# Modulation transposes issued as a later step, and the last head's gate products moved ahead of the third scan's drain

## The chip, the cores and the metric

The kernel runs on one core of one Trainium2 chip. Time is device time in microseconds (us) from start to end of one execution; several executions are timed and the median is given. The engines are TensorE (PE, with its weight loads as PEld), VectorE (DVE), ScalarE (ACT), GpSimd (POOL) and SyncE (SP), which issues nearly all loads.

## The reference, cut to what matters

Two layers run over 128 context tokens and 512 latent tokens, with a model width of 1024. Each layer is a SwiGLU block, a mixer and a second SwiGLU block, each behind a norm with a scale, a shift and a gate that come from a conditioning vector (two of them: one for context, one for latent tokens).

```python
def adaln_params(cond, w, b):                 # w is 1024 x 9216 in each layer
    m = jax.nn.silu(cond) @ w + b
    return m.reshape(cond.shape[0], N_MOD, 1, D_MODEL)      # nine slots: shift, scale, gate, three times

def swiglu(h, w_in, w_out):
    gt, up = jnp.split(h @ w_in, 2, axis=-1)
    return (jax.nn.silu(gt) * up) @ w_out

# even layer: mixer = [conv module || two-way HGRN2 scan of four heads], one projection in, one out
    o = o_f + rev(o_b)
    o = rms_norm(o, norm_g) * jax.nn.silu(g.reshape(B, T, HG_HEADS, HG_VDIM))
    out = jnp.concatenate([a, r], axis=-1) @ w_out
```

The odd layer's mixer is windowed attention; the change doesn't touch it.

## The kernel before

All activations stay on the chip, transposed: feature on the partition, 640 tokens along the row. Products are made in a split form: each fp32 operand is cut into a high and a low part (`split_x`: a cast on ACT, a subtraction on DVE), and three matmuls stand for one. A SwiGLU block (`ffn`) makes its first two hidden tiles j plainly (`plain_pair`) and the others by a Strassen-like scheme: seven products i of 12 matmuls for each j (`strassen`), in the order 1, 5, 6, 2, 7, 3, 4. For the first two such j (2 and 3) the order is interleaved: (2,1) (2,2) (3,1) (3,2) (2,5) (2,6) (2,3) (2,7) (3,5) (2,4) (3,6) (3,3) (3,7) (4,1) (3,4) and so on. After four groups of tiles (6, 6, 6 and 4) `project_out` makes the second product of the block.

The modulation vectors are made beside this work, in two ways.

- `mod_piece` makes a quarter of a slot with TensorE: eight matmuls from two raw weight tiles of 512 KB, a copy from PSUM on ACT (L326), two transposes on PE (L328) and a reduction on DVE (L330). Twelve quarters are tied to hidden tiles j = 2 to 5 of the first three SwiGLU blocks (`pieces`), and are issued behind product i = 4 of that j. Eight more run at the very start.
- `mod_slot` makes a whole slot on DVE: eight steps (`mod_step`, four multiply-adds on DVE each) and then `mod_sum`: 8 matmuls (L357), a copy on ACT (L362), two transposes (L364), and a copy on DVE (L366). These steps are fillers: `plan` spreads them over points in the block by their count, 46, 36 and 36 in the first three blocks. There are 13 such slots.

Raw weights, whatever they are for, pass through one pool of four tiles (`rawp`, allocated in `load_w`), and SP issues their loads in the order of the allocations. A raw tile is free when its last reader is done; for a Strassen pair that is a sum of raw halves on DVE (L742) or a cast of the last half.

The order of the instructions on an engine comes from a list scheduler which takes the program's order as priority and goes on with later instructions where its own model says that earlier ones aren't ready. Loads are drawn ahead by a fixed number of places.

The even mixer is written out by hand in `EVEN_ORDER`: `q` are a head's query and forget projections, `g` its gate projection (48 matmuls in two chunks of 256 and 384 tokens), `s` registers a head's scan, `d` drains the scans up to a head, `m06` and `m68` are the output projection over the inputs 0 to 5 (conv, heads 0 and 1) and 6 to 7 (heads 2 and 3). A scan is a generator of 14 steps: set-up, `dg`, seven levels, `kt`, `kv`, `o`, `rs` (sums of squares, L414), and `hgb` (the inverse root is spread over the partitions by transposes, L457, and multiplied in, L1212). `tick` lets one step go behind a chunk of projection if the counter `pe_time` has grown by STEP since the last one; each step's matmuls are tied behind the last product issued:

```python
    def tick(self):
        if self.scans and self.pe_time - self.stepped >= STEP:      # STEP = 2800
            self.stepped = self.pe_time
            self.step(self.scans)
```

A chunk of `m06` adds 1475 (256 tokens) or 2212 (384 tokens), a gate chunk 1966 or 2949; a level adds 2000 more, `kt` 900, `kv` 1800 and `o` 2800. `m06` has 16 chunks of 18 matmuls. `mix_out` splits the mixer's outputs first (L610) and then multiplies; for `m68` each tile takes input 6 first and input 7 (head 3) second.

Of the kernel before, what the change touches and what calls it, by code (L numbers as in the profile page):

```python
# [8 lines left out]
F32 = mybir.dt.float32  # L9
# [7 lines left out]
P = 128  # L17
D = 1024
KD = D // P
# [26 lines left out]
STEP, NORM_STEP = 2800, 3500  # L46
SPLIT_AHEAD = 100
EPS = 1e-6
EVEN_ORDER = "b0 a0 a1 q0 s0 c1 g0 q1 d0 s1 c2 g1 c3 n0 q2 d1 s2 v1 g2 q3 d2 s3 g3 x0 e0 m06 d3 m68".split()
NEG = -1.0e30  # L50

R_COND, R_BMOD, R_NG, R_CB, R_CG, R_CLB, R_LB, R_HG, R_QK, R_CW = 0, 16, 160, 208, 212, 216, 220, 244, 245, 247
# [23 lines left out]
def run(steps):  # L76
    for _ in steps:
        pass


class Trunk:
# [232 lines left out]
    def mod_piece(self, l, slot, q):  # L314


        nc = self.nc
        ps = self.aux(f"mps{l}_{slot}_{q}")
        for kh in range(2):
            raw = self.load_w(self.i["w_mod"][l, kh * 512:(kh + 1) * 512, slot * D + q * 256:slot * D + (q + 1) * 256],  # L320
                              f"wm{l}_{slot}_{q}_{kh}")
            for j in range(4):
                nc.tensor.matmul(ps[32 * j:32 * j + 32, 0:256], lhsT=self.cond32[:, kh * 4 + j, :], rhs=raw[:, j, :],
                                 start=(kh == 0), stop=(kh == 1), tile_position=(0, 32 * j), skip_group_check=True)
        sb = self.tmp.tile([P, 512], F32, tag="tmp", name=f"msb{l}_{slot}_{q}")[:, 0:256]
        nc.scalar.copy(out=sb, in_=ps[:, 0:256])  # L326
        for t in range(2):
            nc.tensor.transpose(ps[:, 256 + t * P:256 + (t + 1) * P], sb[:, t * P:(t + 1) * P], self.ident)  # L328
        ks = slice(2 * q, 2 * q + 2)
        nc.vector.tensor_reduce(out=self.modv[l][:, slot, ks, :],  # L330
                                in_=ps[:, 256:512].rearrange("p (t j c) -> p t c j", j=4, c=32)[:, :, 0:2, :],
                                axis=AX.X, op=ALU.add)
        self.mod_use(l, slot, ks)
# [17 lines left out]
    def mod_sum(self, l, slot):  # L351
        nc = self.nc
        ps = self.ps("mod", f"mps{l}_{slot}")
        acc = self.mod_acc.pop((l, slot))
        for c in range(2):
            for j in range(4):
                nc.tensor.matmul(ps[32 * j:32 * j + 32, 0:256], lhsT=self.pick[:, 1 - c:33 - c],  # L357
                                 rhs=acc[c][j // 2][:, (j % 2) * 256:(j % 2 + 1) * 256],
                                 start=(c == 0), stop=(c == 1), tile_position=(0, 32 * j), skip_group_check=True)
        self.free(*[f"ma{slot}_{c}_{j}" for c in range(2) for j in range(2)])  # L360
        sb = self.tmp.tile([P, 512], F32, tag="tmp", name=f"msb{l}_{slot}")[:, 0:256]
        nc.scalar.copy(out=sb, in_=ps[:, 0:256])  # L362
        for t in range(2):
            nc.tensor.transpose(ps[:, 256 + t * P:256 + (t + 1) * P], sb[:, t * P:(t + 1) * P], self.ident)  # L364
        src = ps[:, 256:512].rearrange("p (t j c) -> p j t c", j=4, c=32)[:, :, :, 0:2]
        nc.vector.tensor_copy(self.modv[l][:, slot].rearrange("p (j t) c -> p j t c", t=2), src)  # L366
        self.mod_use(l, slot, slice(0, KD))

    def mod_use(self, l, slot, ks):
# [13 lines left out]
                                    op0=ALU.mult)  # L383

    def mod_slot(self, l, slot):
        return [(lambda k=k: self.mod_step(l, slot, k)) for k in range(KD)] + [lambda: self.mod_sum(l, slot)]


    def square_into(self, k, c0, n, c):
# [222 lines left out]
    def product(self, *args):  # L612
        run(self.product_steps(*args))
# [32 lines left out]
    def ffn(self, l, which, n, last):  # L646


        w_out = self.i["ffn_w_out"][l, which]
        pairs = {}  # L650
        mm = self.bank["mm"]
        ring = {"b": mm[0:3], "c": mm[3:5], "a": mm[5:6]}
        g = {}

        def bank(kind, name):
            ring[kind].append(ring[kind].pop(0))
            return self.psum.tile([P, 512], F32, tag=f"bank{ring[kind][-1]}", name=name)[:, 0:HW]

        def do(j, i):
            p = pairs.setdefault(j, dict(done=set()))  # L660
            for r, nm in enumerate(("gate", "up")):
                if nm not in p and (r == 0 or i not in (1, 2)):
                    p[nm] = self.load_w(*self.ffn_first(l, which, j)[r])
            self.strassen(p, j, i, bank, g)

        plain = EARLY if n == 0 else PLAIN
        order = [(j, c) for j in range(plain) for c in range(2)]
        if n:
            order.sort(key=lambda x: x[1])
        weights = {}  # L670
        for j, c in order:
            if j not in weights:
                weights[j] = [(self.weights(*x), x[1]) for x in self.ffn_first(l, which, j)]
            self.plain_pair(j, c, weights[j], g)
        self.free(*[f"b12_{q}" for q in range(4)])
        for q in range(4):
            self.norm_sums(q)
        jobs, ends = [], {}
        for part, (f0, fn) in enumerate(PARTS):
            js = list(range(f0, f0 + fn))  # L680
            if part == 0:
                js = js[plain:]
                first = js[:FIRST_TWO]
                jobs += [(j, i) for j in first for i in (1, 2)]
                jobs += [(first[0], i) for i in (5, 6, 3, 7)]
                for j, nxt in zip(first, first[1:]):
                    jobs += [(nxt, 5), (j, 4), (nxt, 6), (nxt, 3), (nxt, 7)]
                nxt = js[FIRST_TWO]
                jobs += [(nxt, 1), (first[-1], 4)] + [(nxt, i) for i in (5, 6, 2, 7, 3, 4)]
                js = js[FIRST_TWO + 1:]  # L690
            jobs += [(j, i) for j in js for i in (1, 5, 6, 2, 7, 3, 4)]
            ends[len(jobs)] = part
        self.points = self.points[plain:]
        for at, (j, i) in enumerate(jobs):
            do(j, i)
            if i == 4:
                self.point()
                if (l, which, j) in self.pieces:
                    self.mod_piece(*self.pieces.pop((l, which, j)))
                    if not self.pieces:  # L700
                        self.free("cond32")
            if at + 1 in ends:
                part = ends[at + 1]
                f0, fn = PARTS[part]
                if part == len(PARTS) - 1:
                    self.free_operand()
                js = range(f0, f0 + fn)
                run(self.project_out(w_out[f0 * P:(f0 + fn) * P, :], [g[j][0] for j in js], [g[j][1] for j in js], n,
                                     final=(part == len(PARTS) - 1), last=last))
                self.free(*[f"g{j}" for j in js])  # L710
        if not last:
            self.norm_chunk(n + 1, 1)
# [502 lines left out]
    def even_mixer(self, n):  # L1215
# [16 lines left out]

        for step in EVEN_ORDER:
            kind, j = step[0], int(step[1:])
# [305 lines left out]
    def run(self):  # L1540
# [7 lines left out]
        pb = self.transpose_x(rows)  # L1548
        for q in (0, 2, 1, 3):
            for s in (1, 0):  # L1550
                self.mod_piece(0, s, q)
            if q == 0:
                for t in range(EARLY):
                    self.upcoming += self.ffn_first(0, 0, t)
                self.prefetch()
            for k in (2 * q, 2 * q + 1):
                for c in range(2):
                    self.norm_pair(0, c, pb[c], k % 4, (k // 4 * 4,))
# [88 lines left out]
```

## Time and profile before

| | us |
|---|---|
| median of three runs | 2525.38 (2523.1 to 2528.88) |
| profiled execution, its own time | 2523.16 |
| span of its trace | 2521.4 |

How to read it: PE's matmuls and weight loads are pipelined, so that busy shares near the full span mean that the engine was never long without work. What counts for the time is where PE stood idle, who released it, and which level of its clock was granted around that. The profiled execution lies 2.2 us under the median of the three runs.

### The profile page before, as it was taken

The numbers are of one execution on the slowest core, as the hardware profiler recorded it, in microseconds if no ns is written. First come the engines' busy times: TensorE is split into PE (matmuls) and PEld (weight loads), VectorE is DVE, ScalarE is ACT, GpSimd is POOL, SyncE is SP. The second block draws the span as 40 slices with busy tenths as digits, with TensorE's granted clock in tenths as the row PEclk, the third lists the DMA queues.
The fourth block names the chain that finished last, engine by engine and source line by source line (L and its number), as shares of the span: only waits on it lengthen the run. The fifth ranks groups of instructions, "written<-read, shape, count | busy, mean of one in ns | idle before, by whom it ended". The sixth has DMA issues, their size and how long they took to land. (4 is left out here: it accounts for less than half of the span.)

```text
span 2521.4 us, 43474 instructions
## 1 busy us (share of the span) xinstructions
PE 2437.3 (97%) x17072; PEld 2347.9 (93%) x17072; DVE 1982.7 (79%) x3750; ACT 1122.1 (45%) x2278; POOL 224.5 (9%) x308
## 2 busy tenths in 40 slices
PE   7999999999989999999999999999999999999999
PEld 5889999998989989999999899999988899999999
DVE  6889888868997678988887788888777868585755
ACT  6425243543234452525255343434556655252533
POOL 0000000104234110000011000000132111000000
PEclk8999999999999999999999999999999999999999
DMA  8453534412111226343440644344300121232322
GB/s 246 123 178 115 150 113 142 142 46 60 55 45 39 78 67 184 107 137 105 138 139 24 193 122 133 112 129 126 100 28 15 35 80 44 75 87 82 89 80 76
DMA packets 378261, 254.53 MB, mean 101 GB/s; under 512 B 9302, under 2 KB 362953, under 8 KB 378057
## 3 DMA queue, kind: packets, MB, share of 16 engines
q1 hardware_dynamic: 373112, 248.35, 33.7%
q10 hardware_dynamic: 4944, 3.41, 0.5%
q8 instruction: 134, 2.20, 0.4%
q14 instruction: 71, 0.57, 0.1%
HBM read 248.32 MB, written 3.41 MB: 100 GB/s over the span
## 5 line engine op out<-in xcount | busy, mean ns | idle before, releaser
L623 PE MATMUL po<-g,whi_o 128*128 128x256 f32 (+2 forms) x2672 | 579.0, 309 | 2.7 <-DVE st L780 1.1
L623 PEld LDWEIGHTS po<-g,whi_o 128*128 128x128 f32 x2672 | 442.8, 188 | 12.3 <-issue 2.9
L623 PE MATMUL po<-g,wlo_o 128*128 128x256 f32 (+2 forms) x1336 | 408.5, 307 | 0.2 <-DVE wlo_o L610 0.2
L814 DVE SCALAR_TENSOR_TENSOR x<-po,modG,x 128x256 f32<-128x256 f32 (+3 forms) x480 | 196.5, 435 | 127.1 <-PE po L623 125.5
L349 DVE SCALAR_TENSOR_TENSOR ma<-raw_wm,cond,ma 128x512 f32<-128x512 f32 x364 | 263.7, 753 | 33.2 <-DMA raw_wm<-in_w_mod 33.0
L609 ACT CAST ws<-S 128x512 fp32r<-128x512 f32 x290 | 180.3, 622 | 222.0 <-DVE S L742 72.9
L609 ACT CAST whi_o<-raw_o 128x768 fp32r<-128x768 f32 (+1 forms) x142 | 110.4, 777 | 351.9 <-PE po L623 220.7
L623 PEld LDWEIGHTS po<-g,wlo_o 128*128 128x128 f32 x1336 | 250.8, 188 | 0.4 <-DVE wlo_o L610 0.4
L773 PE MATMUL pb<-tdhi,ws 128*128 128x320 f32 x960 | 222.9, 312 | 5.8 <-DVE st L784 4.9
L610 DVE TENSOR_TENSOR ws<-S,ws 128x512 fp32r<-128x512 f32 x290 | 199.1, 688 | 31.5 <-ACT ws L609 30.7
L773 PE MATMUL pc<-b,ws 128*128 128x320 f32 x1140 | 191.2, 309 | 0.0
L773 PE MATMUL pb<-tdlo,ws 128*128 128x320 f32 x600 | 184.9, 309 | 0.0
L773 PEld LDWEIGHTS pb<-tdhi,ws 128*128 128x128 f32 x960 | 162.2, 188 | 13.3 <-DVE st L784 9.6
L773 PEld LDWEIGHTS pc<-b,ws 128*128 128x128 f32 x1140 | 173.4, 188 | 0.0
L405 POOL TENSOR_TENSOR acc<-acc,sq 128x320 f32<-128x320 f32 (+2 forms) x38 | 37.6, 991 | 1351.4 <-ACT sq L404 955.5
L610 DVE TENSOR_TENSOR wlo_o<-raw_o,whi_o 128x768 fp32r<-128x768 f32 (+1 forms) x142 | 126.4, 890 | 30.8 <-ACT whi_o L609 18.9
L773 PE MATMUL pb<-b,ws 128*128 128x320 f32 x700 | 145.7, 309 | 0.8 <-DVE x L814 0.8
L609 ACT CAST ws<-raw_wg 128x512 fp32r<-128x512 f32 x160 | 98.9, 620 | 81.6 <-PE po L623 32.3
L610 DVE TENSOR_TENSOR ws<-raw_wg,ws 128x512 fp32r<-128x512 f32 x160 | 109.8, 688 | 27.8 <-ACT ws L609 27.7
L976 DVE SCALAR_TENSOR_TENSOR cw<-pad,vecs,cw 128x655 f32<-128x655 f32 x120 | 121.5, 1014 | 1.8
L773 PE MATMUL pb<-tclo,ws 128*128 128x320 f32 x400 | 122.2, 308 | 0.0
L773 PE MATMUL pa<-bchi,ws 128*128 128x320 f32 x520 | 116.2, 310 | 6.0 <-DVE st L784 6.0
(509 smaller groups left out, 5742.8 us busy)
## 6 DMA issues: line engine op xcount, KB each, us to landing
raw_wm<-in_w_mod SPq DMA_DIRECT2D x144, 512.0 KB, 4.0
raw_wg<-in_ffn_w_in SPq DMA_DIRECT2D x88, 512.0 KB, 4.1
raw_wu<-in_ffn_w_in SPq DMA_DIRECT2D x88, 512.0 KB, 4.0
raw_o<-in_ffn_w_out SPq DMA_DIRECT2D x96, 384.0 KB, 3.5
raw_o<-in_ffn_w_out SPq DMA_DIRECT2D x32, 256.0 KB, 3.0
raw_z<-in_ev_w_in SPq DMA_DIRECT2D x8, 512.0 KB, 3.9
raw_oq<-in_od_w_in SPq DMA_DIRECT2D x8, 512.0 KB, 5.0
raw_o<-in_od_w_out SPq DMA_DIRECT2D x16, 256.0 KB, 3.0
```

The source lines that it names most:

```text
L349: nc.vector.scalar_tensor_tensor(out=acc, in0=part, scalar=col, in1=acc, op0=ALU.mult, op1=ALU.add)
L405: nc.gpsimd.tensor_tensor(out=self.acc[:, c0:c0 + n], in0=self.acc[:, c0:c0 + n], in1=sq[:, 0:n], op=ALU.add)
L609: nc.scalar.copy(out=hi, in_=src)
L610: nc.vector.tensor_tensor(out=lo, in0=src, in1=hi.bitcast(F32), op=ALU.subtract)
L623: self.last_mm = nc.tensor.matmul(ps, lhsT=a[k], rhs=b[k][:, c0:c0 + n], start=(k == 0 and j == 0), stop=(k == nk - 1 and j == 2))
L773: nc.tensor.matmul(ps, lhsT=a, rhs=b, start=(i in (1, 5, 2) and k == 0 and t == 0), stop=(k == 3 and t == 2), skip_group_check=True)
L814: nc.vector.scalar_tensor_tensor(out=xs, in0=ps[:, s0 - c0:s0 - c0 + sn], scalar=self.modG[:, n, m, g:g + 1], in1=xs, op0=ALU.mult, op1=AL ...
L976: nc.vector.scalar_tensor_tensor(out=y, in0=x[:, j:j + T + 15], scalar=col(j), in1=y, op0=ALU.mult, op1=ALU.add)
```

## The change

`mod_piece` now ends behind the copy on ACT and returns the rest (transposes, reduction, use) as a function. In a block's loop it is called behind product i = 6 of its j, and the returned function behind i = 4, four products later. At the start it is called at once, as before. `mod_sum` is cut likewise: the transposes and what follows become a filler of their own, `mod_last`, so that a slot has ten fillers (51, 40 and 40 in all). The copy's target becomes a slot of the large pool. In `EVEN_ORDER`, `g3` moves from behind `d2 s3` to ahead of them.

```diff
-EVEN_ORDER = "b0 a0 a1 q0 s0 c1 g0 q1 d0 s1 c2 g1 c3 n0 q2 d1 s2 v1 g2 q3 d2 s3 g3 x0 e0 m06 d3 m68".split()
+EVEN_ORDER = "b0 a0 a1 q0 s0 c1 g0 q1 d0 s1 c2 g1 c3 n0 q2 d1 s2 v1 g2 q3 g3 d2 s3 x0 e0 m06 d3 m68".split()
...
         nc.scalar.copy(out=sb, in_=ps[:, 0:256])
+        return lambda: self.mod_turn(l, slot, q, ps, sb)
+
+    def mod_turn(self, l, slot, q, ps, sb):
+        nc = self.nc
         for t in range(2):
             nc.tensor.transpose(ps[:, 256 + t * P:256 + (t + 1) * P], sb[:, t * P:(t + 1) * P], self.ident)
...
-        sb = self.tmp.tile([P, 512], F32, tag="tmp", name=f"msb{l}_{slot}")[:, 0:256]
+        sb = self.slot(f"msb{l}_{slot}", n=256)
         nc.scalar.copy(out=sb, in_=ps[:, 0:256])
+        self.mod_acc[l, slot] = ps, sb
+
+    def mod_last(self, l, slot):
+        nc = self.nc
+        ps, sb = self.mod_acc.pop((l, slot))
         for t in range(2):
             nc.tensor.transpose(ps[:, 256 + t * P:256 + (t + 1) * P], sb[:, t * P:(t + 1) * P], self.ident)
...
+        self.free(f"msb{l}_{slot}")
...
-        return [(lambda k=k: self.mod_step(l, slot, k)) for k in range(KD)] + [lambda: self.mod_sum(l, slot)]
+        return ([(lambda k=k: self.mod_step(l, slot, k)) for k in range(KD)]
+                + [lambda: self.mod_sum(l, slot), lambda: self.mod_last(l, slot)])
...
+        turn = None
         for at, (j, i) in enumerate(jobs):
             do(j, i)
+            if i == 6 and (l, which, j) in self.pieces:
+                turn = self.mod_piece(*self.pieces.pop((l, which, j)))
+                if not self.pieces:
+                    self.free("cond32")
             if i == 4:
                 self.point()
-                if (l, which, j) in self.pieces:
-                    self.mod_piece(*self.pieces.pop((l, which, j)))
-                    if not self.pieces:
-                        self.free("cond32")
+                if turn:
+                    turn()
+                turn = None
...
-                self.mod_piece(0, s, q)
+                self.mod_piece(0, s, q)()
```

## Rows read from the trace of the kernel before

**Rows 1.** The page: each engine's busy time, share of the span, instructions.

```profile
PE 2437.3 (97%) x17072; PEld 2347.9 (93%) x17072; DVE 1982.7 (79%) x3750; ACT 1122.1 (45%) x2278; POOL 224.5 (9%) x308
```

**Rows 2.** Waits of PE: who waited for whom; us, times, longest.

```profile
PE hgb L457 <- DVE r_hg L437: 10.7, 3, 6.4
...
PE mps L328 <- ACT msb L326: 6.1, 8, 1.1
...
PE mps L364 <- ACT msb L362: 3.2, 4, 1.2
```

**Rows 3.** Timeline of PE around one quarter; start, length, in brackets idle before.

```profile
1411.70 1.07 PE L323 MATMUL mps<-raw_wm,cond 128*32 128x256 f32 x16
...
1414.70 0.44 PE L328 MATMUL mps<-ident,msb 128*128 128x128 f32 x2 [1.14 <-ACT msb L326]
```

**Rows 4.** Busy time in a stretch: PE, PEld, DVE, ACT, POOL; granted clock; DMA.

```profile
80.00:128.00 48.00, 46.40 (x347) 43.14 (x349) 36.69 (x75) 22.45 (x48) 0.00 (x0) 1.00 0.58 173
```

**Rows 5.** PE, output products (L623) alone, around the last head's hgb.

```profile
842.70:848.00 5.30, 5.28 (x36) 5.13 (x36) 1.00 0.33 93
848.40:853.71 5.31, 5.26 (x36) 5.29 (x37) 1.00 1.02 276
```

**Rows 6.** Timeline: last head's rs, inverse root, hgb, scaling and split.

```profile
841.69 1.17 PE L414 MATMUL rs_hg<-ones_v,osq 128*128 128x1 f32 x10
...
843.38 0.16 DVE L432 TENSOR_SCALAR root_hg<-r_hg 128x5 int32<-128x5 int32 x1
...
847.99 0.71 PE L457 MATMUL hgb<-ident,r_hg 128*128 128x128 f32 x5
...
850.02 0.73 ACT L609 CAST m<-og 128x640 fp32r<-128x640 f32 x1
...
850.78 0.83 DVE L610 TENSOR_TENSOR m<-og,m 128x640 fp32r<-128x640 f32 x1 [0.32 <-ACT m L609]
```

**Rows 7.** Timeline of DVE: the conv's inverse root, first and last of ten.

```profile
771.40 0.16 DVE L432 TENSOR_SCALAR root_cv<-r_cv 128x5 int32<-128x5 int32 x1
...
773.20 0.17 DVE L437 SCALAR_TENSOR_TENSOR r_cv<-root_cv 128x5 f32<-128x5 f32 x1
```

**Rows 8.** Timeline: third head's rs on PE, inverse root on DVE, hgb on PE.

```profile
789.31 1.05 PE L414 MATMUL rs_hg<-ones_v,osq 128*128 128x1 f32 x8
...
790.70 0.97 DVE L432 TENSOR_SCALAR root_hg<-r_hg 128x5 int32<-128x5 int32 x1
...
795.50 1.27 PE L457 MATMUL hgb<-ident,r_hg 128*128 128x128 f32 x5 [1.99 <-DVE r_hg L437]
```

**Rows 9.** Stretches around hgb of the second and third head, columns as before.

```profile
718.24:724.00 5.76, 5.76 (x27) 5.76 (x28) 5.29 (x6) 0.10 (x1) 3.89 (x6) 0.51 0.00 0
...
793.50:795.50 2.00, 0.01 (x1) 0.00 (x1) 1.84 (x4) 0.59 (x2) 1.71 (x2) 1.00 0.00 0
795.50:799.00 3.50, 3.50 (x14) 3.50 (x15) 2.00 (x4) 0.73 (x1) 0.00 (x0) 0.51 0.00 0
```

**Rows 10.** SP's load issues from the mixer's end into the second SwiGLU block.

```profile
856.63 3.02 SPq L567 DMA_DIRECT2D raw_wu<-in_ffn_w_in  x2
922.01 4.59 SPq L567 DMA_DIRECT2D raw_wm<-in_w_mod  x2
```

**Rows 11.** Timeline of PE: products (3,2), (2,3), (3,5) of that block begin.

```profile
914.52 0.41 PE L773 MATMUL pa<-bchi,ws 128*128 128x320 f32 x1 [1.55 <-DVE st L784]
...
922.84 1.92 PE L773 MATMUL pc<-b,ws 128*128 128x320 f32 x12
...
926.37 0.31 PE L773 MATMUL pc<-tchi,ws 128*128 128x320 f32 x1
```

**Rows 12.** The page: splits (busy us, mean ns) and load issues (us to landing).

```profile
L609 ACT CAST ws<-S 128x512 fp32r<-128x512 f32 x290 | 180.3, 622 | 222.0 <-DVE S L742 72.9
...
L610 DVE TENSOR_TENSOR ws<-S,ws 128x512 fp32r<-128x512 f32 x290 | 199.1, 688 | 31.5 <-ACT ws L609 30.7
...
raw_wu<-in_ffn_w_in SPq DMA_DIRECT2D x88, 512.0 KB, 4.0
```

## Prediction

> **What bounds the kernel now.** I read the page first: PE is busy for 97% of the span [rows 1], so a change gains only what takes idle time from PE, and any PE idle time that it adds is paid in full. The list of PE's waits comes next, because the change names two of them. Transposes of the quarters wait for the copy on ACT 8 times, 6.1 us in all; those of the whole slots 4 times, 3.2 us [rows 2]. The timeline around one quarter shows the mechanism: eight matmuls of 1.0 us, a few products that the scheduler slips in, then the transposes, 1.14 us too early because the copy stood behind other work on ACT [rows 3]. So 12 of the 25 places wait at all; the others are already covered. The third view is the even mixer around the gate and the scans, for the second edit. There the transposes `hgb` wait for the inverse root on DVE three times, 10.7 us in all [rows 2]; the last head's `hgb` does not wait.
>
> **Quarters.** Four products now stand between copy and transposes, 4 x 1.76 us (two products take 922.84 to 926.37 [rows 11]). The longest wait was 1.1 us [rows 2]. All 6.1 us should go. DVE could be late next, but it is busy for 36.7 of 48 us where four quarters lie [rows 4], so it can follow: -6.1 us, and nothing if it could not.
>
> **Whole slots.** The wait goes where the new filler falls to a later point. Working `plan` through with 51, 40 and 40 fillers, 10 of 13 slots get `mod_last` at a later point; three (slot 3 of the first block, slot 4 of the second, slot 6 of the third) have both in one point and stay as before. The old rate was 4 waits in 13 places of 0.8 us each, so three such places keep 3 x 4/13 x 0.8 = 0.7 us. Gain 3.2 - 0.7 = 2.5 us; bounds -3.2 (none waits) and +0.4 (all three wait 1.2). That fillers move by a place or two I take at nothing: the same steps and the same loads lie in the same blocks, and DVE has room [rows 4].
>
> **The gate.** `g3` brings 48 matmuls wherever it stands; what moves is which scan step stands behind which chunk. I counted `pe_time` through both orders. Before: `d2` drains the third head's last four steps, the gate's two chunks let go the last head's first two steps, and its `hgb` falls behind chunk 14 of the 16 of `m06`. The trace agrees: 36 matmuls (two chunks of 18) lie between `rs` and `hgb` and 36 more between `hgb` and the end of `m06` [rows 5]. After: the gate's chunks let go `kv` and `o` of the third head, all 14 steps of the last head start in `m06`, `o` falls behind chunk 15, `rs` behind chunk 16, and `hgb` is drained with nothing left of `m06`. `m68` needs that head as its second input. So the cover is gone, and PE waits through a chain that it now gets for free:
> - end of `rs` to the first DVE operation: 842.86 to 843.38, 0.5 us [rows 6]. The ten operations of the inverse root take 771.40 to 773.37, 2.0 us, with DVE free [rows 7]; together 2.5. For the third head, `rs` to `hgb` took 790.36 to 795.50, 5.1 us [rows 8]. I take 3.8: DVE has output tiles and weight splits between.
> - end of `hgb` to both parts of the split: 848.70 to 851.61, 2.9 us [rows 6]; at best 2.5, and the high part, with which a product can begin, is there 0.86 earlier (850.75). I take 2.8.
> - against it, the first half of `m68`'s tiles needs only head 2: three matmuls of 0.147 us a tile (1.76/12), 0.4 us for one tile, 2.6 for all six banks. I take 1.3, three tiles.
>
> Idle: 3.8 + 2.8 - 1.3 = 5.3 us, between 2.5 + 2.5 - 2.6 = 2.4 and 5.1 + 2.9 - 0.4 = 7.6.
>
> **The clock behind it.** After the 2.0 us wait at 793.5 the granted clock was 0.51, the lower level of 1.2 GHz, for 3.5 us of work, and at 718 for 5.8 us [rows 9]; around the transposes' short waits it stayed at 1.00 [rows 4]. Work at half clock costs half its time: 1.7 to 2.9 us. I take 1.7. The gate therefore costs 7.0 us, between 4.1 and 10.5.
>
> The Trainium skill (TensorE: Matmul & The Clock Gate, "Why this matters for your kernels") warns against idle gaps between bursts of matmuls, because the clock falls back. This is the rule that speaks against the change, and the rows agree with it. If the clock did not fall, the sum below would be lower by 1.7 us, that is -2.3.
>
> The slow inverse root of the third head has a cause that matters for the 3.8. Its first operation took 0.97 us against 0.16 elsewhere [rows 7, 8], while POOL was busy for 1.71 of 2.00 us [rows 9]. The Trainium skill (SBUF — State Buffer, "Who interferes with whom") says that DVE operations with two inputs from SBUF, or in a two-port mode, and GpSimd's reads block each other. By it the chain would be 2.5 us wherever POOL rests, and the sum -1.9; by the contended row it would be 5.1 us, and the sum +0.7.
>
> **Loads.** All four raw tiles hold weights long before the Strassen part: the last `up` half is issued by 859.7, and no load follows until 922.01 [rows 10]. By allocation order the fourth is the `up` half of j = 3. With the quarter moved ahead of (3,5), both its raw tiles come before that half. One takes the fourth buffer, the other waits for the first release (922.0), and the `up` half for the quarter's first matmuls, some 0.5 us behind (2,6), which ends where (2,3) begins, 922.84 [rows 11]. Issue 923.4, landing 4.0 us later, sum 0.69, cast 0.62, subtraction 0.69 [rows 12]: ready at 929.4. PE would reach (3,5) at 926.37 + 1.0 for the quarter = 927.4, so it is 2.0 us late; if (2,4) is drawn ahead, 0.3. That is 0.9 to 6.0 us over three blocks. On the other side, PE's idle 1.5 us ahead of (3,2) [rows 11] may take the quarter's first half, 0.5 us a block: -1.5. I take +1.0, near the end where the scheduler swaps, since it swaps often. Later pairs gain room, because quarters free their buffers four products earlier. A quarter's PSUM bank is now reused one product (1.76 us) after the last transposes; the reduction behind them takes 0.17 us and I take that as hidden.
>
> **Sum.** -6.1 - 2.5 + 7.0 + 1.0 = -0.6 us on the profiled execution's 2523.2, that is 2522.6; that execution lies 2.2 under the median, so by the median 2525.4 - 0.6 = 2524.8 us.
>
> **Rivals.**
> - *The end of the scan stays covered.* If the scheduler finds work for PE while the last head is finished, the gate costs nothing: -6.1 - 2.5 + 1.0 = -7.6, 2517.8 us. For it: the scheduler mixes streams freely, and all six banks of first halves are 2.6 us. Against it: each step's matmuls are tied behind the last product, and nothing but `m68` is left. 0.20. A milder form, in which the third head's 2.0 us wait and its half clock (1.7) vanish, gives -0.6 - 3.7 = -4.3, 2521 us; POOL's work has no tie to the gate, so I give it 0.08, half of it beyond the bound.
> - *The half-loaded pair, on the other side.* The `up` half of j = 3 comes 2.0 us late in three blocks: -0.6 - 1.0 + 6.0 = +4.4; with the chain at its dear end (10.5) +7.9, 2533.3 us. The kernel is slower at all from 0.5 us a block, and by over 5 us from 2.2 a block at the gate's middle price, from 1.0 at its dear end. For it: the pool is full for 62 us ahead of that pair [rows 10], and loads go out in the order of allocation. Against it: (2,4) is ready by then. 0.20.
> - *The change does not do what it says.* The scheduler puts the transposes where its model has them ready, so they could wait elsewhere; then only the costs stay, +8.0, 2533.4 us. Against it: four products are six times the longest wait. 0.04.
>
> **How the numbers follow.** The forecast, all terms near their middle, has 0.48. A measurement here tells about 0.2%, 5 us, from no change. Faster by more: 0.20 + 0.04 and a tail of the forecast, 0.27. Slower by more: 0.20 + 0.04, less the part of the rival that stays within, 0.22. The same: 0.51. The range goes to the bounds of both sides, 2516 (everything gained, a cheap chain) to 2533; the forecast's own is 2520 to 2530.
>
> **What would show it.** PE's waits on `msb` should fall to under 1 us. `hgb` should wait for the inverse root once more than before, some 3 us, and the first product of `m68` for the split of `m`, with a granted clock near 0.5 behind it. The first load of a quarter in a block should be issued before that of the second `up` half, and (3,5) show a wait on a sum of raw halves. Wrong would be: `m68` beginning without a wait, waits on `msb` still there, or new waits of the quarters' matmuls on their loads.

## The result, and the profile after

The changed kernel takes 2548.53 us (median of four runs, 2546.14 to 2551.45); the kernel before, timed beside it, 2524.7 (2523.1 to 2528.88). The ratio is 1.0096 (95% interval 1.008 to 1.0111): 24 us slower, where 2524.8 with a range to 2533 was forecast. The profiled execution took 2551.45 us.

Line numbers from L327 on are higher than before by 4 to 15: `hgb` is L468, the slot's sum L361, the output products L634, the Strassen products L788. The page's first part, to be held against [rows 1]:

```profile
PE 2457.3 (96%) x17072; PEld 2358.0 (92%) x17072; DVE 1983.6 (78%) x3750; ACT 1121.5 (44%) x2278; POOL 226.4 (9%) x308
```

The span grew by 28.2 us, of which 20.0 are busy time of PE for the same 17072 matmuls and only some 8 idle time. The lower clock explains most of the busy time but not all of it: span times granted clock (0.989 before, 0.984 after) puts some 13 us of the growth to the clock; what else lengthens it isn't traced. The waits of PE (who for whom; us, times, longest), against [rows 2]:

```profile
PE hgb L468 <- DVE r_hg L448: 11.6, 3, 6.4
PE mps L323 <- DMA raw_wm<-in_w_mod: 11.0, 10, 4.2
PE pb L788 <- DVE st L799: 8.2, 11, 2.5
...
PE rs_n L425 <- POOL acc L416: 3.0, 2, 2.5
...
PE po L634 <- ACT m L620: 2.7, 1, 2.7
...
PE mps L361 <- DVE ma L353: 2.4, 1, 2.4
```

No row for a transpose's wait on `msb`, the target of the copy, is left: the edit does what it says. But the quarters now wait more often for their loads (11.0 us in 10 waits). The kernel before had two such waits, both at its very start:

```profile
PE mps L323 <- DMA raw_wm<-in_w_mod: 5.9, 2, 5.5
```

The scan's end, the norm behind it and a slot's sum show waits of 2.4 to 2.7 us each. Setting the start of each matmul of one trace beside the same one of the other shows where the 28.2 us arise: +13.2 between 778 and 918 us of before (last scans, `m68` and what follows it), +4.4 and +8.4 in the first Strassen products of the second and the third block (918 to 976, 1371 to 1513), +7.7 up to 199. Between 199 and 508 it is 5.4 us faster.

The scan's end, timeline of PE, against [rows 6]:

```profile
856.83 1.17 PE L425 MATMUL rs_hg<-ones_v,osq 128*128 128x1 f32 x10
...
859.43 0.89 PE L634 MATMUL po<-m,o 128*128 128x320 f32 x5
860.38 0.76 PE L468 MATMUL hgb<-ident,r_hg 128*128 128x128 f32 x5
863.80 0.56 PE L634 MATMUL po<-m,whi_o 128*128 128x320 f32 x2 [2.66 <-ACT m L620]
...
872.91 0.58 PE L425 MATMUL rs_n<-ones_d,acc 128*128 128x1 f32 x2 [2.48 <-POOL acc L416]
```

From `rs` to `hgb` PE is busy with first halves of `m68` (15 matmuls, 857.86 to 860.3). From `hgb` to the split it is idle for 2.66 us, as foreseen. The wait of 2.48 us for the norm's sums was not: the tiles of `m68` come out late and close together, so the norm's sums on GpSimd end 2.48 us after PE's last product. Three stretches (columns as in [rows 4]): behind the slot's sum that waited for VectorE until 162.92, around the last `hgb`, and behind the wait of the norm's sums:

```profile
162.92:169.40 6.48, 6.48 (x26) 3.60 (x26) 3.37 (x7) 0.83 (x1) 0.00 (x0) 0.50 0.65 210
856.00:864.00 8.00, 5.28 (x37) 4.77 (x36) 5.65 (x18) 2.44 (x4) 0.00 (x0) 1.00 0.83 217
872.91:886.31 13.40, 13.40 (x57) 13.36 (x58) 3.80 (x11) 2.80 (x7) 1.41 (x2) 0.50 0.13 39
```

13.4 us at a granted clock of 0.50, the lower level, cost 6.7 us. The kernel before has two shorter stretches at that place, which cost half as much:

```profile
867.30:870.70 3.40, 3.40 (x15) 3.40 (x15) 2.44 (x7) 2.23 (x5) 1.73 (x2) 0.50 0.00 0
884.30:887.70 3.40, 3.40 (x16) 3.40 (x16) 2.28 (x8) 1.86 (x3) 0.00 (x0) 0.51 0.00 0
```

The start of the second block. SP's queue first, then PE:

```profile
872.16 66.86 SPq L578 DMA_DIRECT2D raw_wm<-in_w_mod  x2
939.12 1.61 SPq L578 DMA_DIRECT2D raw_wu<-in_ffn_w_in  x1
```
```profile
942.81 0.64 PE L323 MATMUL mps<-raw_wm,cond 128*32 128x256 f32 x8 [1.08 <-DMA raw_wm<-in_w_mod]
...
946.83 0.42 PE L788 MATMUL pc<-tchi,ws 128*128 128x320 f32 x1 [0.62 <-ACT ws L620]
```

One row holds the quarter's two loads: the first goes out at 872.16 and takes the fourth raw tile, the second stands in the queue until one is free, some 67 us later, and PE waits 1.08 us for it. The `up` half of j = 3 is issued behind it at 939.12, and (3,5) waits 0.62.

### The profile page after: what moved, and what is told of

Read it like the earlier page. It is cut to its first block, busy times and chain, and to the rows that moved or that the text cites. A ratio compares the mean times of both kernels' runs of the same rounds, so it can differ in the third digit from the quotient of the medians.

```text
span 2549.6 us, 43446 instructions
## 1 busy us (share of the span) xinstructions
PE 2457.3 (96%) x17072; PEld 2358.0 (92%) x17072; DVE 1983.6 (78%) x3750; ACT 1121.5 (44%) x2278; POOL 226.4 (9%) x308
## 5 line engine op out<-in xcount | busy, mean ns | idle before, releaser
L634 PE MATMUL po<-g,whi_o 128*128 128x256 f32 (+2 forms) x2672 | 580.2, 309 | 4.7 <-ACT g L620 3.5
L634 PEld LDWEIGHTS po<-g,whi_o 128*128 128x128 f32 x2672 | 443.1, 188 | 16.6 <-issue 4.9
L634 PE MATMUL po<-g,wlo_o 128*128 128x256 f32 (+2 forms) x1336 | 409.7, 307 | 0.2 <-DVE wlo_o L621 0.2
L353 DVE SCALAR_TENSOR_TENSOR ma<-raw_wm,cond,ma 128x512 f32<-128x512 f32 x364 | 262.4, 749 | 28.4 <-DMA raw_wm<-in_w_mod 28.2
L634 PEld LDWEIGHTS po<-g,wlo_o 128*128 128x128 f32 x1336 | 251.4, 188 | 2.1 <-issue 1.6
L788 PE MATMUL pb<-tdhi,ws 128*128 128x320 f32 x960 | 224.3, 314 | 10.0 <-DVE st L799 8.2
L788 PE MATMUL pc<-b,ws 128*128 128x320 f32 x1140 | 192.5, 310 | 0.0
L788 PE MATMUL pb<-tdlo,ws 128*128 128x320 f32 x600 | 184.8, 309 | 0.0
L788 PEld LDWEIGHTS pb<-tdhi,ws 128*128 128x128 f32 x960 | 163.0, 189 | 18.3 <-DVE st L799 11.2
L788 PEld LDWEIGHTS pc<-b,ws 128*128 128x128 f32 x1140 | 173.6, 188 | 3.3 <-issue 1.6
L788 PE MATMUL pb<-b,ws 128*128 128x320 f32 x700 | 145.1, 309 | 0.3 <-DVE x L829 0.3
L788 PE MATMUL pa<-bchi,ws 128*128 128x320 f32 x520 | 117.5, 313 | 6.4 <-DVE st L799 6.4
L788 PE MATMUL pb<-tclo,ws 128*128 128x320 f32 x400 | 122.2, 308 | 0.0
```

What stands on the lines that cost most here:

```text
L353: nc.vector.scalar_tensor_tensor(out=acc, in0=part, scalar=col, in1=acc, op0=ALU.mult, op1=ALU.add)
L634: self.last_mm = nc.tensor.matmul(ps, lhsT=a[k], rhs=b[k][:, c0:c0 + n], start=(k == 0 and j == 0), stop=(k == nk - 1 and j == 2))
L788: nc.tensor.matmul(ps, lhsT=a, rhs=b, start=(i in (1, 5, 2) and k == 0 and t == 0), stop=(k == 3 and t == 2), skip_group_check=True)
```

## The experiments

All 18 versions were timed against the kernel before. A difference in us below is the ratio less one, times 2527.

### The parts alone

`e1` has only the new `EVEN_ORDER`, `e2` all but that, `e3` only the quarters, `e4` only the slots.

> The kernel before with the new place of the last head's gate products alone. Theory A (the gate's place costs most of the 24 us: with the products gone from the third scan's end nothing covers the last head's norm and the scan's drain, TensorE waits there and stands longer at the lower clock): 11 to 14 us above the kernel before, since the stretch from 778 to 926 us of before grew by 13.2 us in the changed kernel, with the waits for the last head's norm rows, for the state written by ScalarE and for the sum written by GpSimd there. Theory B (no part costs much alone; the cost comes from the places at which the shifted filler steps fall): within 4 us of the kernel before, and the 24 us show only where the parts are together.

> The changed kernel with the gate products at their old place. Theory A: the two other parts leave 10 to 13 us above the kernel before (24 less the gate's 11 to 14): the quarters' loads that come a moment late at the start of the second and third blocks, and the longer time at the lower clock there. Theory B: 20 us and more, as the shifted steps are all still shifted.

> The kernel before with the quarters of the modulation alone moved ahead and their transposes made a later step. Theory A: the waits for the quarters' evictions are gone (6 us less), the quarters wait for their own loads instead (the rows of the changed kernel: 11.0 us in 10 waits where it had 5.9 us in 2, so 5 us more), and a start of a block at the lower clock costs 2 to 7 us: 0 to 8 us above. Theory C (the slots in whole, with one more filler step each, cost what is not the gate's): 2 to 6 us below the kernel before.

> The kernel before with the whole slots' sums and transposes alone made two filler steps. Theory A: the 13 waits for the slots' evictions are gone (2.5 us), one sum waits for VectorE 2.4 us and then falls to the lower clock (3.4 us): within 4 us of the kernel before. Theory C: 8 to 14 us above, since every later filler stands one to thirteen places later than it was planned.

| version | ratio (95% interval) | us |
|---|---|---|
| e1, gate alone | 1.0047 (1.0025 to 1.007) | +12 |
| e2, quarters and slots | 1.004 (1.0025 to 1.0055) | +10 |
| e3, quarters alone | 1.0028 (1.0012 to 1.0043) | +7 |
| e4, slots alone | 0.9988 (0.9977 to 0.9999) | -3 |

Theory A holds for the gate, and the slots gain what was forecast. The quarters, forecast at -5.1 us with their loads, cost 7. Slots and quarters together cost 10, not 7 - 3 = 4; the three intervals leave room for some 6 us of error, so that something lies between the two is likely here, and e9 below bears it out.

Each result also gives the span and the mean granted clock. Span times clock is the span if all of it ran at the full clock; the rest is lost to the clock. On average 17 runs of before give 2496.7 and 29.1 us, six of e1 2504.4 and 33.4, four of the changed kernel 2507.9 and 38.8. So the gate costs 7.7 us of work and waits and 4.3 of clock, the latter within the scatter of the six runs; all together 11.2 and 9.7.

### The gate's place: cover

`e8` keeps the gate's new place, but in `m06` a scan step goes behind every chunk:

```diff
-        if self.scans and self.pe_time - self.stepped >= STEP:
+        if self.scans and self.pe_time - self.stepped >= self.stride:
...
+            self.stride = 1400 if step == "m06" else STEP
```

> The kernel before with the gate's products at their new place, and during the first part of the mixer's output projection a scan step behind every chunk (by a bound of 1400 in place of 2800), so that by the counters the last head's transposes fall behind chunk 14 of 16 as in the kernel before. Theory A (the cost is the lost cover at the scan's end): within 3 us of the kernel before, with no wait of the first product of the second projection for the split of the head. Theory B (the cost comes from what the gate's products displace at their new place, or from the third head's end): 8 us and more above the kernel before.

Measured: 1.0012 (1.0001 to 1.0023), +3 us instead of +12. The scan's end in its trace (PE) and the stretch around it:

```profile
850.95 1.17 PE L414 MATMUL rs_hg<-ones_v,osq 128*128 128x1 f32 x10
...
855.89 0.76 PE L457 MATMUL hgb<-ident,r_hg 128*128 128x128 f32 x5
```
```profile
848.00:856.00 8.00, 8.00 (x61) 7.87 (x61) 6.26 (x21) 3.67 (x9) 0.00 (x0) 1.00 0.32 88
856.00:864.00 8.00, 8.00 (x55) 7.87 (x56) 5.65 (x13) 3.98 (x6) 0.00 (x0) 1.00 0.94 259
```

PE is busy for all 16 us and keeps its clock, as before the change [rows 5]. So about 9 of the 12 us are the lost cover, known to some 6 us by the two intervals. The stretch at the lower clock goes with it: the traces of e1 and e14, both with the gate at its new place and the cover lost, have 0.50 for 13.4 us there too (from 878.9 and 862.9), e8's has only two short stretches, as before (0.50 for some 3.3 us from 875.1 and from 892.2). What stays is at the third head, whose end the gate's place also moves: `m06` begins with waits of 0.27 and 0.94 us for the splits, and `hgb` waits 2.79 where it waited 1.99 [rows 8].

### The quarters: gain and cost apart

```diff
 # e5: matmuls stay behind i = 4, transposes behind i = 6 of the next pair
+            if i == 6 and turn:
+                turn()
+                turn = None
 # e6: all of it behind i = 6
+                self.mod_piece(*self.pieces.pop((l, which, j)))()
 # e7: as in the change, but j = 2 at its old place
-            if i == 6 and (l, which, j) in self.pieces:
+            if i == (4 if j == 2 else 6) and (l, which, j) in self.pieces:
```

> The kernel before with only the transposes of the quarters moved: loads and matmuls stay behind product 4 of their pair, the transposes stand behind product 6 of the next pair; the last quarter of a block, ahead of the output projection, stays whole. Theory A (the waits on the copies were worth what they showed; what costs is that the quarters' matmuls and loads moved): 3 to 6 us below the kernel before. Theory B (those waits were time in which VectorE caught up; without them TensorE waits as long for the products' operands): within 1.5 us of it.

> The kernel before with the quarters moved whole to behind product 6: loads, matmuls, copy and transposes together, so that the waits for the copy stay. Theory A: the cost of the moved loads and matmuls without the gain, 9 to 13 us above the kernel before. Theory B: what the quarters alone cost, 5 to 7 us above.

> The quarters moved as in the change, but the first quarter of each of the three blocks at its old place. Theory A (the first quarter's loads find no free buffer so early in the block): 4 to 6 us below the kernel with all quarters moved, so within 2 us of the kernel before; no wait of a block's first quarter for its load in the list of TensorE's waits. Theory B: 0 to 2 us below the kernel with all quarters moved.

Measured: e5 0.9998 (0.9986 to 1.001), e6 1.0028 (1.0019 to 1.0038), e7 1.0002 (0.9991 to 1.0012); that is -0.5, +7 and +0.5 us. Neither theory is right as a whole. The cost is A's: moved matmuls and loads cost 7 us with or without the delay of the transposes (e6, e3), and the three first quarters of the blocks are all of it (e7); in e7's trace they wait for no load. But e6 doesn't show the cost without the gain, as it was meant to: at the new place most of the waits for the copy were gone as well (1.7 us in 4, where before has 6.1 in 8). The gain is B's: without the waits for the copy the time falls by nothing that these runs can tell from none. PE's waits in e5:

```profile
PE mps L323 <- DMA raw_wm<-in_w_mod: 7.8, 7, 5.0
...
PE pb L784 <- DVE st L795: 5.9, 12, 2.0
...
PE pb L784 <- ACT ws L613: 3.7, 2, 2.8
...
PE mps L332 <- ACT msb L326: 0.6, 1, 0.6
```

6.1 us of waits for `msb` became 0.6, and other waits took their place (`pb` for a cast of weights, 3.7, has no row before). The quarter of [rows 3] shows how: ACT and PE in e5,

```profile
1412.76 0.62 ACT L613 CAST ws<-raw_wg 128x512 fp32r<-128x512 f32 x1 [3.89 <-DMA raw_wg<-in_ffn_w_in]
```
```profile
1409.53 1.07 PE L323 MATMUL mps<-raw_wm,cond 128*32 128x256 f32 x16
1413.43 0.56 PE L784 MATMUL pb<-bchi,ws 128*128 128x320 f32 x2 [2.83 <-ACT ws L613]
```

PE begins the quarter at 1409.53, 2.2 us earlier than before, is through with it at 1410.6, and then waits 2.83 us for the next pair's first weights: ACT had been idle for 3.89 us until `raw_wg` landed. Behind the wait for the copy stood a load, at this place. How far one trace's list of waits can be trusted: the whole slots' waits for `msb`, which neither e1 nor e5 touches, are 3.2 us before, 5.2 in e1 and 5.9 in e5.

Span times clock says more than the time: e5's runs have 2494.2 us of waits and work on average, where before beside them has 2498.3. So 4 us did go (to within 1.5), and 29.6 us lost to the clock against 27.3 took part of it back, though that difference is within the scatter (2.5).

### Both repairs, and the parts that gain

> The changed kernel with both repairs: the first quarter of each block back at its old place, and a scan step behind every chunk of the mixer's first projection. Theory A (the two costs found are all that there is): the sum of what the parts cost alone, gate with repair 3, quarters with repair 0 to 1, slots -3: within 3 us of the kernel before. Theory D (the parts together cost more than each alone, as the 24 us against 12 + 6 - 3 = 15 say): 6 to 10 us above the kernel before.

> The kernel before with the whole slots' transposes as a filler of their own and the quarters' transposes alone moved to the next pair, gate and quarters' matmuls at their old places. If the two parts add up: 3 to 5 us below the kernel before, the fastest of the versions. If the waits on TensorE only change their names: 0 to 3 us below it.

Measured: e9 1.0037 (1.0025 to 1.005), +9 us; e10 0.9991 (0.9981 to 1), -2 us. Theory D holds: with both repairs a remainder stays that no part has alone. e10 is in the range of waits that only change their names, but slots and late transposes alone, -3 and -0.5, add up to nearly as much. One of the two long waits of e9's trace that before lacks is at 1502.57, in the third block (PE, DVE, SP):

```profile
1502.57 0.63 PE L788 MATMUL pb<-tdhi,ws 128*128 128x320 f32 x1 [2.68 <-DVE st L799]
```
```profile
1501.43 0.69 DVE L757 TENSOR_TENSOR S<-raw_wg,raw_wu 128x512 f32<-128x512 f32 x1 [1.73 <-DMA raw_wu<-in_ffn_w_in]
```
```profile
1494.58 0.53 SPq L578 DMA_DIRECT2D raw_wu<-in_ffn_w_in  x1
```

The row of PE names `st`, but `st` (1502.04) stands on VectorE behind a sum that waited for `raw_wu`, issued at 1494.58 and there only at 1501.43. Again a load. The other, 2.66 us until 157.65 in the first block, is a slot's sum that waits for VectorE, and in the 8 us ahead of it VectorE waits for no load.

### The loads

`e11` and `e12` take the slots' loads away (before, and e5). Their output is another, as the expectation says.

```diff
-        w = self.load_w(self.i["w_mod"][l, k * P:(k + 1) * P, slot * D:(slot + 1) * D], f"wm{l}_{slot}_{k}")
...
-                acc, part = self.mod_acc[l, slot][c][j], w[:, 0, j * 512:(j + 1) * 512]
+                acc, part = self.mod_acc[l, slot][c][j], self.X[2 * j + c][:, 0:512]
```

> The kernel before without the loads of the whole slots' weights: each filler step takes tiles of the residual in their place, so VectorE's work stays and 104 loads of 0.5 MB, with the raw tiles that they occupy, are gone; the output is another. For comparison with the next run. If the load of the next pair's weights sets the pace where the quarters lie, 10 us and more below the kernel before; if it doesn't, 0 to 5 us below.

> The same without the slots' loads, and with the quarters' transposes alone moved to the next pair. Theory L (behind the wait for a quarter's copy stood the wait for the next pair's weights, which the slots' loads delay): now the gain comes out, 4 to 6 us below the run before it. Theory V (VectorE is what TensorE waits for in that stretch; its work is unchanged): within 2 us of the run before it.

Measured: 0.995 (0.9939 to 0.9962) and 0.9943 (0.993 to 0.9956), -13 and -14 us. The slots' loads, or the raw tiles that they hold, do cost time: VectorE's work is unchanged. By span times clock 18 us of waits and work went in e11, and 6 more were lost to the clock. The gain of the late transposes, 2 us, is in Theory V's range and within the intervals. L's 4 to 6 could not have come out whole: the waits for `msb` are 7.4 us in e11's trace, and 3.9 stay in e12's.

The last six runs have five raw tiles; the room comes from one of 16 pairs of working tiles:

```diff
-N_PAIRS, N_SLOTS, N_WIDE = 16, 18, 6
+N_PAIRS, N_SLOTS, N_WIDE = 15, 18, 6
-        self.rawp = pool("raw", 4)
+        self.rawp = pool("raw", 5)
```

> The kernel before with five raw tiles for loaded weights in place of four (the room taken from one of the 16 pairs of working tiles). For comparison with the three runs behind it. If loads that wait for a tile hold TensorE up in the kernel before too, 2 to 6 us below it; the missing pair may cost some of that.

> The changed kernel with five raw tiles. Theory L (quarters moved ahead and slots with one more step ask for one of four raw tiles at moments when none is free, and what is late then is a load): the gate's part is left, 8 to 13 us above the kernel before with five tiles. Theory D (the cost lies in what the engines do and wait for among themselves): 19 to 24 us above it, as with four tiles.

> The changed kernel with the gate's products at their old place, and five raw tiles. Theory L: 3 us above to 5 us below the kernel before with five tiles, where it was 8 above with four. Theory D: 6 to 9 us above.

> The changed kernel with both repairs and five raw tiles. Theory L: within 3 us of the kernel before with five tiles, where it was 9 above with four. Theory D: 7 to 10 us above.

| five raw tiles | ratio (95% interval) | us above e13 | with four tiles |
|---|---|---|---|
| e13, before | 0.9961 (0.9947 to 0.9975) | | |
| e14, changed | 1.0018 (1.0006 to 1.003) | 14 | 24 |
| e15, gate at its old place | 0.9974 (0.9961 to 0.9987) | 3 | 10 |
| e16, both repairs | 0.9977 (0.9964 to 0.999) | 4 | 9 |

By the two intervals such a difference is known to some 5 us. Theory L holds, with e14 and e16 a microsecond outside its ranges: the gate's part stays (14 - 3 = 11 us), and of the 10 us of quarters and slots 3 are left. PE's waits for loads and for the norm in e14:

```profile
PE mps L323 <- DMA raw_wm<-in_w_mod: 4.9, 2, 4.5
PE rs_n L425 <- POOL acc L416: 2.7, 2, 2.3
```

Two waits for `raw_wm` are left, both at the kernel's very start, and the slot's sum has no longer wait than 0.5; the wait of the norm is that of the lost cover. That the kernel before also gains 10 us by the fifth tile says how much its own loads hold it up.

> Five raw tiles, and of the change only the quarters' transposes behind product 6 of the next pair. Theory L (with four tiles the wait for the next pair's weights took the place of the wait for the copy): 3 to 5 us below the kernel before with five tiles, so 13 to 15 below the kernel before. Theory V (VectorE and ScalarE keep TensorE waiting as long in any case): within 2 us of the kernel before with five tiles.

> Five raw tiles, the quarters' transposes alone moved, and the whole slots' transposes as a filler of their own; gate and quarters' matmuls at their old places. If the parts add up on top of the fifth tile: 13 to 16 us below the kernel before, the fastest version. If the waits only change their names: 9 to 12 us below.

Measured: e17 0.997 (0.9956 to 0.9984), -8 us; e18 0.9951 (0.9935 to 0.9967), -12 us. e17 is 2 us above e13, near V's range, but settles little: with five tiles the waits for `msb` are only 3.2 us before the edit (e13), and 2.6 stay in e17 at the last quarters of the blocks, whose transposes it leaves in place. e18 has the lowest ratio of the versions that leave no work out, and beats both kernels; its distance to e13, 2.5 us, is within the intervals.

## Why the prediction was wrong, by its own steps

- **Quarters, -6.1: the step failed.** That the waits would go was right (none is left). That time would go with them rested on VectorE being "busy for 36.7 of 48 us where four quarters lie [rows 4], so it can follow". The share of a stretch says nothing of what PE needs next, and VectorE wasn't it: at the place of [rows 3] PE met the landing of the next pair's weights. With the transposes alone moved, -0.5 us (interval -3.5 to +2.5), where span times clock has, on average, 4 less of waits and work and 2 more lost to the clock. That a load takes over is shown at this place; what takes over at the others is not settled, and e12, without the slots' loads, didn't bring the rest of the gain out.
- **Loads, +1.0 with a bound of +6.0: mis-sized and partly misplaced.** The mechanism was foreseen (four tiles full, the second half of the quarter and the `up` half of j = 3 behind it). But the quarter itself waits first, for its second half: 1.57, 1.08 and 0.58 us in the three blocks, and the `up` half then costs 0.62 in the second. The step held only (3,5) to be late, and took the value near the end where the scheduler swaps. Its credit of 1.5 us didn't come: PE's wait ahead of (3,2) in the second block stayed, 1.98 us where it was 1.55. New waits of the quarters on their loads were the prediction's own sign of being wrong, and they came. The move of matmuls and loads costs 7 us (e6, e3), all of it in the first quarters (e7); the waits named here are about 4 of them, and where the rest arises is open.
- **Whole slots, -2.5: right.** -3 us alone. "That fillers move by a place or two I take at nothing" holds alone (one sum waits for VectorE there too, 1.7 us) and not beside the moved quarters: together 6 us more than the sum. There the trace names VectorE (2.36 us until 162.92); with a fifth tile that wait is gone (0.3 in e15), so the room for loads is behind it. The interaction of two edits in one pool had no term.
- **Gate, +7.0 with a bound of +10.5: mechanism right, size low.** 12 alone. Of the idle 5.3 us at the scan's end the sum came out (2.66 + 2.48 = 5.1), but by luck, since the parts didn't: the way from the end of `rs` to `hgb` was 2.4 us and all covered by first halves, where 3.8 less 1.3 was taken, and the norm's sums on GpSimd came late, which wasn't thought of. The clock took 6.7 us there where it took 3.4 before, so 3.3, not 1.7. Waits at the third head, 2 us more than before, were not in the sum at all.
- **The rivals.** Of the rivals whose signs came, the half-loaded pair with the gate at its dear end was nearest (2533), but no term or rival added the clock to the waits of loads, or the slots to the quarters. The mean of four runs against 17 of before gives 9.7 us lost to the clock beside 11.2 of waits and work; the sum had 1.7.

The Trainium skill (TensorE: Matmul & The Clock Gate, "Why this matters for your kernels") warns of idle gaps between bursts of matmuls. The trace agrees in part: behind the 2.48 us wait the granted clock was 0.50 for 13.4 us, while behind the longer wait of 2.66 us, until 863.80, it was still 0.98 on average from 864 to 872.9. The Trainium skill's other rule (SBUF — State Buffer, "Who interferes with whom") is borne out where it could be: with POOL idle (0.00 of 8 us in the stretch from 856) the chain from `rs` to `hgb` took 2.4 us, 858.0 to 860.38, where the prediction's lower bound is 2.5. POOL isn't all that counts: in e14's trace it is idle there too, but a split of weights (1.22 us) stands ahead of the chain on VectorE, the chain takes 3.1 us, and `hgb` waits 0.79 us.

## What to carry to other kernels

A wait in the list is worth its time only if what PE does next is ready: look at the place for the operation behind the wait, and for the load it needs, before counting the wait as gain. Set time lost to waits and time lost to the clock apart, by span times granted clock, since one can hide the other. Work that moves ahead takes its loads along, and in a full pool it moves everything allocated behind it. Work that stands at the end of a chain may be the chain's cover: count what is left for PE when the last step of the chain runs, up to the last sum of the norm behind it.

## What the runs showed of the hardware that was not expected

The mean granted clock of one program varies between its executions, and with it the time: six runs of e1 range from 2529.6 us at 0.990 to 2548.5 at 0.983, while the kernel before, beside it, ranges from 2522.6 to 2532.4 at 0.986 to 0.990. One execution of e1 could have been read as +2 us, another as +21; why this program varies more, no run here tells.
